# Layer B of a two-layer decoder step: one plain pair of value tiles instead of two, finer steps for the norms ahead of it

## The chip, the core and the metric

One core of a Trainium2 chip runs the whole step in one launch. The metric is the device time of an execution in microseconds. Five engines work from queues of their own: TensorE (PE; its weight loads are PEld), VectorE (DVE), ScalarE (ACT), GpSimd (POOL) and SyncE (SP), which here issues all DMAs. An engine takes its instructions in the order of its queue, and an instruction waits at the head until what it needs is there.

## The reference

Two layers over 1024 prompt tokens and 8 single-token samples, 1032 columns, with a model width of 1024. Layer A is a gated linear recurrence, layer B a gated MLP with spatial mixing. Each layer ends in a per-layer embedding (PLE): a gate from the normed residual times a projection of p.

```python
def chunk_mlp_mixer(h, w_in, ln_g, ln_b, w_sp, b_sp, w_out):
    proj = h @ w_in
    u, v, z = jnp.split(proj, 3, axis=-1)
    u = jax.nn.gelu(u)
    v = layernorm(jax.nn.gelu(v), ln_g, ln_b)
    ...
    y = (u * s * jax.nn.silu(z)) @ w_out
    ...
for i in range(DEPTH):
    hn = rmsnorm(h, norm_mix[i])
    ...
    h = h + y
    gate = jax.nn.sigmoid(rmsnorm(h, norm_ple[i]) @ w_ple_gate[i])
    h = h + gate * (p[i] @ w_ple_proj[i])
```

The change lies where layer A ends and layer B begins: the end of the first gate (i = 0), the second norm of the residual for layer B, the p projection of layer B, and the first tiles of the value branch v.

## The kernel before

**Layout.** Features lie on the partitions, tokens in the free dimension, in three chunks c = 0, 1, 2 of 384, 384 and 264 columns (`OFF`, `W`). A float32 operand is split into a high part in fp32r and a rest (`split`, `split_weights`: the cast is on ACT, the subtraction on DVE or, for every other activation row, on POOL). A product of two such operands is three matmuls (`mm3`: high times high, high times rest, rest times high). A plain output tile of 128 features and one chunk is therefore 8 blocks of depth times 3, or 24 matmuls (`proj`). The split weights of a tile are `whi` and `wlo`, two buffers each, so the cast for the next tile but one waits for the last matmul of the tile that holds the buffer.

**Units.** Most of layer B's input projection runs in units of two output tiles (`unit`): the columns of chunks 0 and 1 and the two halves of the depth make a 2x2 block product, computed by Winograd's scheme in seven products of 12 matmuls instead of eight. Chunk 2 is done plainly (`last`). A unit needs sums of weight blocks (`load_unit`: s1 to s4, four sums on POOL and four more splits `shi`, `slo`), sums of the normed rows (`mix`: the tiles xm, `xmh` and `xml`, three of them, made on DVE from the rows of chunks 0 and 1), and the sum `hr[0][j+4]`, split into the first half of chunk 1's normed tile once its plain readers are done. The first two pairs of value tiles run plainly, because the sums do not exist yet.

**Order.** PE's order is the order in which the code is written. Side work is written as generators, and `tk.tick()` advances all of them by a step; a generator that yields a number sleeps for so many steps. So the number of steps between two pieces decides how many matmuls stand between them in PE's queue. In `proj` there was a step after the fourth of eight blocks, and callers add one at the end of a group: two steps per group of 24. On ACT, DVE, POOL and SP a scheduler sets the order from what the code issues and its priorities.

**The norm between the layers.** When a chunk's last two gate groups are written (`ple`, the pair with m = 6 and 7), `norm_rows` is spawned for that chunk with two numbers from `NDEL[1]`. After the first, `norm_sum` writes small matmuls (`pss`) that sum the squares over the partitions, an addition on DVE (`rms_e`) and a power on POOL (`rsq`). After the second, `norm_bc` writes the matmuls that spread the result over the partitions (`pbc`), and then the eight rows of the chunk are scaled on DVE, cast on ACT (`bh`) and subtracted on DVE and POOL in turns (`bl`). The sum of squares `ssq` of a chunk gets its last addend on DVE (from `sql`, a square on ACT).

**What stands around it on PE.** The last pair of gate tiles; the first half of layer B's p projection (`pple`: 12 products of 6 matmuls, each copied out by ACT as `pple_t` and stored), then the plain value pairs, then the units. The loop around `pple` gave a step for every other product:

```python
for i, _ in enumerate(pple(1, ph, pl, 0, places([(pq, "pple_t", 8)]))):
    if i % 2:
        tk.tick()
```

Behind the first plain pair, a loop ticked until all `norm_rows` were done, and `mix` was spawned there; behind the second, a loop ticked until `mix` was done, and the first unit's weights were loaded.

Of the kernel before, what the change touches and what calls it, by code (L numbers as in the profile page):

```python
# [24 lines left out]
MI = DI // P  # L25
# [11 lines left out]
DL = 4  # L37
KB = 1
SDEL = ((6, 3), (6, 2), (4, 2))
NDEL = (((1, 2), (1, 3), (2, 2)), ((2, 2), (2, 4), (3, 3)))  # L40
OFF = (0, 384, 768)
W = (384, 384, 264)
NT = (3, 3, 2)
CH = (0, 1, 2)
# [36 lines left out]
def trunk_kernel(ctx, tc, xT, st, pT, nrm, wina, lbl, gna, wouta, winb, lng, lnb, lngr, lnbr,  # L81
# [5 lines left out]
    tk = Ticks()  # L87
# [33 lines left out]
    order = [("p", 0, 0)]  # L121
# [7 lines left out]
    order += [("oa", m, f) for m, f in half_order]  # L129
    order += [("g", 0, m) for m in range(KT)]  # L130
    order += [("p", 1, 0)]
    order += [("b", MI + m) for m in range(4)] + [("B", MI + m) for m in range(4, MI, 2)]
    for g in range(8):
        order += [("B", 2 * g), ("B", 2 * MI + 2 * g)]
    order += [("p", 1, 1)]
# [7 lines left out]
    def split_weights(src, width, names, pl):  # L143
        hi = pl.tile([P, width], F32R, name=names[0], **names[2])
        lo = pl.tile([P, width], F32R, name=names[1], **names[2])
        A.copy(hi, src)  # L146
        V.tensor_tensor(lo, src, hi.bitcast(F32), ALU.subtract)  # L147
        return hi, lo
# [6 lines left out]
    def fetch_weights(n):  # L155
        src = wsrc[order[n][0]]
        for i in order[n][1:]:
            src = src[i]
        staged[n] = wp.tile([P, 1024], F32, name="wstg")
        nc.sync.dma_start(staged[n], src)  # L160

    def load(n, wait=False):
        if n >= len(order) or n in loaded or wait and order[n][0] == "B":
            return
        if order[n][0] == "B":
            loaded[n] = load_unit(order[n][1])
            return
        if n not in staged:
            fetch_weights(n)
        stg = staged.pop(n)  # L170
        with tc.high_priority(offset=PRI if order[n][:2] == ("p", 1) or order[n][0] == "b" else 0):
            loaded[n] = split_weights(stg, 1024, PLAIN, wp)
# [27 lines left out]
    taken = [0]  # L200

    def take(*key):
        n = taken[0]
        assert order[n] == key, (order[n], key)
        load(n)
        load(n + 1, key[0] == "b")
        taken[0] += 1
        return loaded[n]


    last, rest = {}, {}

    def split(hi, lo, src, eng=V):
        last["split"] = A.copy(hi, src)  # L214
        last["lo"] = eng.tensor_tensor(lo, src, hi.bitcast(F32), ALU.subtract)  # L215
# [82 lines left out]
    def proj(wt, xh, xl, c):  # L298

        wh, wl = wt  # L300
        ps = pp.tile([P, 512], F32, name="ps_proj", tag="mm", bufs=3)
        for k in range(KT):
            mm3(ps[:, :W[c]], blk(wh, k), blk(wl, k), xh[:, k, :], xl[:, k, :], k == 0, k == KT - 1)
            if k == 3:
                tk.tick()
        return ps

# [9 lines left out]
    def places(stg):  # L317

        n = [0]

        def place(c, mm):
            pl_, tag, bufs = stg[n[0] % len(stg)]
            n[0] += 1
            return pl_.tile([P, 384], F32, name="pple_t", tag=tag, bufs=bufs)[:, :W[c]]
        return place

    def pple(l, ph, pl, half, place):

        wh, wl = take("p", l, half)
        for c in CH:  # L330
            for mm in range(4):
                ps = pp.tile([P, 512], F32, name="ps_pple", tag="mm", bufs=3)
                for k in range(2):
                    b = 2 * mm + k
                    mm3(ps[:, :W[c]], blk(wh, b), blk(wl, b), ph[c][:, k, :], pl[c][:, k, :], k == 0, k == 1)
                t = place(c, mm)
                with tc.high_priority(offset=PRI if l else 0):
                    last["pple"] = A.copy(t, ps[:, :W[c]])  # L338
                nc.sync.dma_start(ppd[l][4 * half + mm][:, OFF[c]:OFF[c] + W[c]], t)
                yield 1  # L340
# [73 lines left out]
    hh, hl = new_act()  # L414
# [11 lines left out]
    ph, pl = [None] * 3, [None] * 3  # L426
# [406 lines left out]
    ph, pl = r["p"]  # L833
# [106 lines left out]
    def ple(l, ep, hh, hl, ssq, done, mid=None):  # L940
        def group(m, c, wg, pj):
            w = W[c]
            pg = proj(wg, hh[c], hl[c], c)
            gt = sp.tile([P, 384], F32, name="tmp", bufs=4)
            with tc.high_priority(offset=PRI if m >= KT - 2 else 0):
                A.activation(gt[:, :w], pg[:, :w], AF.Sigmoid)
                V.tensor_tensor(gt[:, :w], gt[:, :w], pj[:, OFF[c]:OFF[c] + w], ALU.mult)
                V.tensor_tensor(hr[c][m], hr[c][m], gt[:, :w], ALU.add)
            accum_sq(sp, ssq[c], hr[c][m], m == 0, m == KT - 1, w)
            if l == 0:  # L950
                nc.sync.dma_start(hd[m][:, OFF[c]:OFF[c] + w], hr[c][m])
            tk.tick()

        def start(m):
            pj = ep.tile([P, T], F32, name="pj", bufs=2)
            nc.sync.dma_start(pj, ppd[l][m])
            return take("g", l, m), pj

        def pair(m):
            a, b = start(m), start(m + 1)  # L960
            for c in CH:
                group(m, c, *a)
                group(m + 1, c, *b)
                if m == KT - 2:
                    done(c)

        pair(0)
        for m in range(2, KT - 2):
            if m == 3 and mid:
                mid()  # L970
            a = start(m)
            for c in CH:
                group(m, c, *a)
        pair(KT - 2)

    def norm_spawn(c, ssq, gi, act, d):
        tk.spawn(norm_proc(sp, ssq[c], lambda j: hr[c][j], gi, act[0][c], act[1][c], c, d[c]))
# [2 lines left out]
    act = new_act()  # L980
    out_phase("oa", zt, ssq, True, lambda c: norm_spawn(c, ssq, 1, act, NDEL[0]), pre,
              [(c, 8, 8) for c in CH], [(c, 8) for c in CH])
# [21 lines left out]
    def mix():  # L1004


        for j in range(4):
            b11, b12, b21, b22 = hr[0][j], hr[1][j], hr[0][j + 4], hr[1][j + 4]
            with tc.issue_after(last["norm"].ins):
                V.tensor_tensor(b11, b12, b11, ALU.subtract)  # L1010
                V.tensor_tensor(b12, b22, b12, ALU.subtract)
                V.tensor_tensor(b22, b22, b11, ALU.subtract)
                V.tensor_tensor(b21, b21, b22, ALU.subtract)
                for i, t in ((1, b22), (0, b11), (2, b12)):
                    split(xm[i][0][:, j, :], xm[i][1][:, j, :], t)
            yield 1

    with ExitStack() as sG:
        ep = pool(sG, "pj")
        ssq2 = new_ssq()  # L1020
        hn = new_act()
        with ExitStack() as s:
            pq = pool(s, "p1", side="right")
            ph, pl = [None] * 3, [None] * 3

            def mid():
                behind = last["split"]
                for c in CH:
                    load_p(pq, 1, c, ph, pl, behind, [x[:, :2, :W[c]] for x in xm[c]])

            ple(0, ep, act[0], act[1], ssq2, lambda c: tk.spawn(norm_rows(c, ssq2, 2, hn, NDEL[1][c])), mid)
            for i, _ in enumerate(pple(1, ph, pl, 0, places([(pq, "pple_t", 8)]))):
                if i % 2:
                    tk.tick()
    hh, hl = hn

    ws[0] = pool(sB, "wsum")
# [11 lines left out]
    def vgroup(m, c, src, d=2):  # L1049
        w = W[c]  # L1050
        gv = wide()
        A.activation(gv[:, :w], src, AF.Gelu_apprx_tanh)
        if c == 2:
            G.tensor_copy(gvs[:, m, :], gv[:, 256:264])
        tk.spawn(vstore(m, c, gv), d)
# [13 lines left out]
        yield  # L1069


    for q in range(0, 4, 2):
        wv = take("b", MI + q), take("b", MI + q + 1)
        for c in CH:
            for m in range(2):
                ps = proj(wv[m], hh[c], hl[c], c)
                vgroup(q + m, c, ps[:, :W[c]], 4)
                tk.tick()
        if q == 0:
            while any(p[2].__name__ == "norm_rows" for p in tk.procs):  # L1080
                tk.tick()
            tk.spawn(mix(), 1)
    while any(p[2].__name__ == "mix" for p in tk.procs):
        tk.tick()
    for j in range(4):
        split(hh[1][:, j, :], hl[1][:, j, :], hr[0][j + 4])
    load(taken[0])
    sH.close()

    wb2 = pool(sB, "workB2", side="right")  # L1090
# [94 lines left out]
        if not early:  # L1185
            last(1)

    for m in range(4, MI, 2):
        unit(take("B", MI + m), lambda i, c, src: vgroup(m + i, c, src), early=m == 4)

    mv = wb.tile([P, 8, 2], F32, name="mv")
    ss_ = wb2.tile([P, MI, NS], F32, name="ss_")
# [90 lines left out]
    for g in range(8):  # L1283
# [15 lines left out]
        else:  # L1299
# [3 lines left out]
            ph, pl = p_in_act(1, None, False)  # L1303
# [13 lines left out]
            def first():  # L1317
# [8 lines left out]
    act3 = new_act()  # L1326
    out_phase("ob", zt, ssq3, False, lambda c: norm_spawn(c, ssq3, 3, act3, NDEL[0]), {},
              [(1, 12, 4), (2, 0, 8)], [[(2, 0), (2, 8)], [(0, 8), (1, 8), (1, 12)]], pple(1, ph, pl, 1, lambda c, mm: hr[c][4 + mm]))
# [106 lines left out]
```

## Time and profile before

| what | value |
|---|---|
| median of three runs | 1916.89 us |
| the three runs | 1912.62, 1918.22, 1916.89 us |
| the profiled execution's own time | 1914.28 us |
| its span, first to last instruction | 1912.4 us |
| mean granted clock of TensorE | 0.993 |
| DVE, ACT, POOL busy | 60%, 42%, 23% of the span |

A row of the timeline gives the start in us from the span's start, the duration, the engine, the line, the operation, output and inputs, their shapes and how many were merged; in brackets stands the idle time of the engine before it and what ended it. A row of the windows gives for each engine its busy time in that stretch with the number of instructions, then the granted clock and the DMA share. Matmuls are pipelined, so a matmul's duration is longer than the distance to the next one's start; what it costs is that distance.

### The profile page before, as it was taken

How to read it: one execution, taken by the hardware profiler on the slowest of the kernel's cores; microseconds unless marked ns; L12 is line 12 of the kernel's file. 1: busy time of each engine (PE TensorE's matmuls, PEld its weight loads, DVE VectorE, ACT ScalarE, POOL GpSimd, SP SyncE). 2: the span in 40 equal slices, each digit the busy share in tenths (PEclk: the TensorE clock that was granted, in tenths of full speed). 3: DMA queues.
4: the chain of work that ended last, by engine and by line, in shares of the span. 5: the costliest groups of instructions: out<-in, count | busy, mean ns of one | idle time of the engine just before them, and what ended most of it. 6: DMA issues, size and time to landing. Idle time of an engine off the chain costs nothing.

```text
span 1912.4 us, 33713 instructions
## 1 busy us (share of the span) xinstructions
PE 1882.9 (98%) x13250; PEld 1856.2 (97%) x13250; DVE 1156.3 (60%) x2610; ACT 800.1 (42%) x1711; POOL 432.8 (23%) x441
## 2 busy tenths in 40 slices
PE   9999999999999999999999999999999999999997
PEld 8999999999999998999999999999999999999997
DVE  5967676766767677411465755577777776311455
ACT  6463544444454546311244544434434335311342
POOL 4110000000010001011233332345445451011321
PEclk8999999999999999999999999999999999999998
DMA  6231323222231326711243343323333236611123
GB/s 214 76 117 61 118 72 103 78 81 78 92 99 60 111 69 191 251 49 51 76 143 117 109 145 99 90 81 106 124 114 106 97 108 197 222 45 45 67 89 111
DMA packets 124302, 203.76 MB, mean 107 GB/s; under 512 B 11568, under 2 KB 97264, under 8 KB 123120
## 3 DMA queue, kind: packets, MB, share of 16 engines
q1 hardware_dynamic: 124144, 201.61, 32.2%
q8 instruction: 104, 1.70, 0.4%
q14 instruction: 54, 0.44, 0.1%
HBM read 148.75 MB, written 52.82 MB: 105 GB/s over the span
## 4 chain that ended last, share of the span: by engine, by line
PE 90%; DVE 5%; DMA 2%; POOL 1%; ACT 1%; issue 1%; SPq 0%; DVEq 0%; ACTq 0%; POOLq 0%
PE ps_proj L219 18%; PE ps_proj L221 18%; PE ps_proj L220 18%; PE ps_o L219 6%; PE ps_o L220 6%; PE ps_o L221 6%; PE ps_d L221 1%; PE ps_d L219 1%; PE ps_d L220 1%; PE psp L1255 1%; PE pC L672 1%; PE pt_o L718 1%; PE p L638 1%; PE pt_g L1061 1%; PE pss L269 1%
## 5 line engine op out<-in xcount | busy, mean ns | idle before, releaser
L219 PE MATMUL ps_proj<-bh,whi 128*128 128x384 f32 (+1 forms) x2160 | 695.1, 322 | 2.1 <-ACT pple_t L338 1.6
L221 PE MATMUL ps_proj<-bh,wlo 128*128 128x384 f32 (+1 forms) x2160 | 679.9, 315 | 0.5 <-DVE wlo L147 0.5
L220 PE MATMUL ps_proj<-bl,whi 128*128 128x384 f32 (+1 forms) x2160 | 678.8, 314 | 1.4 <-POOL bl L215 1.4
L219 PEld LDWEIGHTS ps_proj<-bh,whi 128*128 128x128 f32 x2160 | 407.4, 189 | 3.6 <-ACT pple_t L338 1.7
L220 PEld LDWEIGHTS ps_proj<-bl,whi 128*128 128x128 f32 x2160 | 407.8, 189 | 2.6 <-POOL bl L215 2.6
L221 PEld LDWEIGHTS ps_proj<-bh,wlo 128*128 128x128 f32 x2160 | 406.5, 188 | 1.7 <-DVE wlo L147 1.7
L147 DVE TENSOR_TENSOR wlo<-wstg,whi 128x1024 fp32r<-128x1024 f32 x148 | 184.8, 1249 | 147.4 <-ACT whi L146 146.2
L146 ACT CAST whi<-wstg 128x1024 fp32r<-128x1024 f32 x148 | 155.0, 1048 | 155.2 <-PE ps_proj L220 104.1
L255 POOL TENSOR_TENSOR ssq<-ssq,tmp 128x384 f32<-128x384 f32 (+1 forms) x72 | 76.3, 1060 | 406.7 <-ACT tmp L254 359.9
L911 DVE TENSOR_TENSOR h<-h,ps_o 128x384 f32<-128x384 f32 (+1 forms) x48 | 24.6, 512 | 192.4 <-PE ps_o L221 190.9
L254 ACT ACTIVATE tmp<-h 128x384 f32<-128x384 f32 (+1 forms) x72 | 35.3, 491 | 219.3 <-DVE h L911 168.9
L219 PE MATMUL ps_o<-bh,whi 128*128 128x384 f32 (+1 forms) x384 | 122.1, 318 | 0.0
L220 PE MATMUL ps_o<-bl,whi 128*128 128x384 f32 (+1 forms) x384 | 121.8, 317 | 0.0
L221 PE MATMUL ps_o<-bh,wlo 128*128 128x384 f32 (+1 forms) x384 | 121.8, 317 | 0.0
L146 ACT CAST shi<-ssum 128x512 fp32r<-128x512 f32 x88 | 54.6, 622 | 110.0 <-PE ps_proj L220 60.2
L219 PE MATMUL ps_o<-zh,whi 128*128 128x384 f32 (+1 forms) x288 | 90.1, 313 | 0.0
L220 PE MATMUL ps_o<-zl,whi 128*128 128x384 f32 (+1 forms) x288 | 89.7, 312 | 0.0
L221 PE MATMUL ps_o<-zh,wlo 128*128 128x384 f32 (+1 forms) x288 | 89.7, 312 | 0.0
L215 POOL TENSOR_TENSOR ql<-q,qh 128x384 fp32r<-128x384 f32 (+1 forms) x24 | 22.4, 931 | 254.5 <-ACT qh L214 254.5
L147 DVE TENSOR_TENSOR slo<-ssum,shi 128x512 fp32r<-128x512 f32 x88 | 68.8, 783 | 12.0 <-ACT shi L146 12.0
L675 DVE TENSOR_TENSOR q<-q,t 128x192 f32<-128x192 f32 (+1 forms) x144 | 47.4, 330 | 44.7 <-PE pC L672 38.3
L219 PEld LDWEIGHTS ps_o<-bh,whi 128*128 128x128 f32 x384 | 72.2, 188 | 0.0
(303 smaller groups left out, 3930.5 us busy)
## 6 DMA issues: line engine op xcount, KB each, us to landing
wstg<-in_wina SPq DMA_DIRECT2D x48, 512.0 KB, 3.7
wstg<-in_winb SPq DMA_DIRECT2D x48, 512.0 KB, 3.7
pj<-ppd SPq DMA_DIRECT2D x16, 516.0 KB, 5.2
S<-in_st SPq DMA_DIRECT2D x16, 512.0 KB, 5.4
vb<-vd SPq DMA_DIRECT2D x16, 512.0 KB, 4.6
out_so_s<-S SPq DMA_DIRECT2D x16, 512.0 KB, 3.4
wstg<-in_wouta SPq DMA_DIRECT2D x16, 512.0 KB, 3.5
wstg<-in_wgate SPq DMA_DIRECT2D x16, 512.0 KB, 3.5
```

Source lines behind the costliest of these rows:

```text
L146: A.copy(hi, src)
L147: V.tensor_tensor(lo, src, hi.bitcast(F32), ALU.subtract)
L215: last["lo"] = eng.tensor_tensor(lo, src, hi.bitcast(F32), ALU.subtract)
L219: PE.matmul(ps, wh, xh, start=first, stop=False, skip_group_check=more)
L220: PE.matmul(ps, wh, xl, start=False, stop=False, skip_group_check=more)
L221: PE.matmul(ps, wl, xh, start=False, stop=last, skip_group_check=more)
L254: A.activation(sq[:, :w], src, AF.Square)
L255: eng.tensor_tensor(ssq, ssq, sq[:, :w], ALU.add)
L269: PE.matmul(pss[:, i:i + 1], t[:, o:o + P], ones[:, 0:1], start=j == 0, stop=j == len(parts) - 1)
L638: PE.matmul(blk(p0, i), blk(Y, i), blk(X, i), start=True, stop=True)
L675: V.tensor_tensor(ql[:, :, 1, :], ql[:, :, 1, :], t2[:, :, 0:1].broadcast_to([P, n, lv]), ALU.mult)
L911: V.tensor_tensor(hr[c][m], hr[c][m], ps[:, :W[c]], ALU.add)
```

## The change

The second plain value pair becomes a unit, so layer B now has one plain pair and seven value units. `mix` is spawned at once, ahead of the only plain pair, and both loops that ticked until work was done are gone. The first unit's weights are loaded after the plain pair's first chunk. In the last pair of the first gate, `proj` gives a step after the second, fourth and sixth block, so that with the caller's step a group of 24 has four; the sleeps of `NDEL[1]` are counted in these. Each p product gives a step.

```diff
-NDEL = (((1, 2), (1, 3), (2, 2)), ((2, 2), (2, 4), (3, 3)))
+NDEL = (((1, 2), (1, 3), (2, 2)), ((3, 2), (5, 3), (3, 3)))
...
-    order += [("b", MI + m) for m in range(4)] + [("B", MI + m) for m in range(4, MI, 2)]
+    order += [("b", MI + m) for m in range(2)] + [("B", MI + m) for m in range(2, MI, 2)]
...
-            if k == 3:
+            if k == 3 or fine[0] and k in (1, 5):
                 tk.tick()
...
+        fine[0] = l == 0
         pair(KT - 2)
+        fine[0] = False
...
-            for i, _ in enumerate(pple(1, ph, pl, 0, places([(pq, "pple_t", 8)]))):
-                if i % 2:
-                    tk.tick()
+            for _ in pple(1, ph, pl, 0, places([(pq, "pple_t", 8)])):
+                tk.tick()
...
-    for q in range(0, 4, 2):
-        wv = take("b", MI + q), take("b", MI + q + 1)
-        for c in CH:
-            for m in range(2):
-                ps = proj(wv[m], hh[c], hl[c], c)
-                vgroup(q + m, c, ps[:, :W[c]], 4)
-                tk.tick()
-        if q == 0:
-            while any(p[2].__name__ == "norm_rows" for p in tk.procs):
-                tk.tick()
-            tk.spawn(mix(), 1)
-    while any(p[2].__name__ == "mix" for p in tk.procs):
-        tk.tick()
+    tk.spawn(mix(), 1)
+    wv = take("b", MI), take("b", MI + 1)
+    for c in CH:
+        for m in range(2):
+            ps = proj(wv[m], hh[c], hl[c], c)
+            vgroup(m, c, ps[:, :W[c]], 4)
+            tk.tick()
+        if c == 0:
+            load(taken[0])
     for j in range(4):
         split(hh[1][:, j, :], hl[1][:, j, :], hr[0][j + 4])
-    load(taken[0])
...
-    for m in range(4, MI, 2):
-        unit(take("B", MI + m), lambda i, c, src: vgroup(m + i, c, src), early=m == 4)
+    for m in range(2, MI, 2):
+        unit(take("B", MI + m), lambda i, c, src: vgroup(m + i, c, src), early=m == 2)
```

**First place: DVE, chunk 1's last addend.** In DVE's queue at the end of the first gate, `ssq_11647` is the sum of squares of chunk 1, `h_7_10170` its last gated row, `h_0_10155` to `h_7_10162` are rows of chunk 0. Before:

```order
L947 TENSOR_TENSOR tmp<-tmp,pj 128x384
L948 TENSOR_TENSOR h_7_10170<-h_7_10170,tmp 128x384
L252 TENSOR_TENSOR ssq_11647<-ssq_11647,sql 128x384
L996 SCALAR_TENSOR_TENSOR h_0_10155<-h_0_10155,g_72,pbc 128x384
L996 SCALAR_TENSOR_TENSOR h_1_10156<-h_1_10156,g_72,pbc 128x384
```

and now:

```order
L949 TENSOR_TENSOR tmp<-tmp,pj 128x384
L1001 SCALAR_TENSOR_TENSOR h_5_10160<-h_5_10160,g_72,pbc 128x384
L950 TENSOR_TENSOR h_7_10170<-h_7_10170,tmp 128x384
L1001 SCALAR_TENSOR_TENSOR h_6_10161<-h_6_10161,g_72,pbc 128x384
L147 TENSOR_TENSOR wlo<-wstg,whi 128x1024
L254 TENSOR_TENSOR ssq_11647<-ssq_11647,sql 128x384
```

Chunk 0's scaled rows have moved ahead of chunk 1's addend, and so has the rest `wlo` of the p weights.

**Second place: DVE, chunk 2's `rms_e`.** Further on in DVE's queue, `h_6_10169` and `h_7_10170` are now rows of chunk 1 being scaled, and `rms_e` is that of chunk 2. Before:

```order
L996 SCALAR_TENSOR_TENSOR h_6_10169<-h_6_10169,g_72,pbc 128x384
L272 TENSOR_SCALAR rms_e<-pss 128x3
L215 TENSOR_TENSOR bl_11653<-h_5_10168,bh_11650 128x384
L996 SCALAR_TENSOR_TENSOR h_7_10170<-h_7_10170,g_72,pbc 128x384
L147 TENSOR_TENSOR wlo<-wstg,whi 128x1024
```

and now:

```order
L1001 SCALAR_TENSOR_TENSOR h_6_10169<-h_6_10169,g_72,pbc 128x384
L1001 SCALAR_TENSOR_TENSOR h_7_10170<-h_7_10170,g_72,pbc 128x384
L217 TENSOR_TENSOR bl_11653<-h_5_10168,bh_11650 128x384
L274 TENSOR_SCALAR rms_e<-pss 128x3
L217 TENSOR_TENSOR bl_11653<-h_7_10170,bh_11650 128x384
```

All eight rows of chunk 1 and three of its four rests now stand ahead of chunk 2's `rms_e`; the `wlo` has moved behind chunk 2's rows.

**Third place: PE, chunk 2's `pbc`.** In PE's queue the matmuls that spread chunk 2's result (`rsq_12769` before, `rsq_12729` now) stood half-way through the first plain group of the value pair (`bh_11649` and `bl_11652` are chunk 0's normed rows). Before:

```order
L219 MATMUL ps_proj<-bh_11649,whi 128x384
L220 MATMUL ps_proj<-bl_11652,whi 128x384
L221 MATMUL ps_proj<-bh_11649,wlo 128x384
L280 MATMUL pbc<-ident,rsq_12769 128x128 x2
L280 MATMUL pbc<-ident,rsq_12769 128x8
```

and now (`xmh_11639` and `xml_11640` hold chunk 1 of p here):

```order
L221 MATMUL ps_pple<-xmh_11639,whi 128x384
L222 MATMUL ps_pple<-xml_11640,whi 128x384
L223 MATMUL ps_pple<-xmh_11639,wlo 128x384
L282 MATMUL pbc<-ident,rsq_12729 128x128 x2
L282 MATMUL pbc<-ident,rsq_12729 128x8
```

They have moved ahead of the last five of the twelve p products. In all PE has 12 matmuls of 384 columns fewer.

More of the change, by code (lines that the diff above doesn't have):

```diff
@@ L211, in trunk_kernel @@
     last, rest = {}, {}
+    fine = [False]
     def split(hi, lo, src, eng=V):
@@ L973, in ple @@
                 group(m, c, *a)
+        fine[0] = l == 0
         pair(KT - 2)
+        fine[0] = False
     def norm_spawn(c, ssq, gi, act, d):
@@ L1069, in vstore @@
         yield
-    for q in range(0, 4, 2):
-        wv = take("b", MI + q), take("b", MI + q + 1)
-        for c in CH:
-            for m in range(2):
-                ps = proj(wv[m], hh[c], hl[c], c)
-                vgroup(q + m, c, ps[:, :W[c]], 4)
-                tk.tick()
-        if q == 0:
-            while any(p[2].__name__ == "norm_rows" for p in tk.procs):
-                tk.tick()
-            tk.spawn(mix(), 1)
-    while any(p[2].__name__ == "mix" for p in tk.procs):
-        tk.tick()
+    tk.spawn(mix(), 1)
[7 more added lines that the diff above has]
+            load(taken[0])
+    assert not any(p[2].__name__ in ("norm_rows", "mix") for p in tk.procs)
     for j in range(4):
         split(hh[1][:, j, :], hl[1][:, j, :], hr[0][j + 4])
-    load(taken[0])
     sH.close()
```

## The prediction

> **What bounds the kernel now.** I read the page first, then the chain of work that ended last, then the windows and PE's timeline from the first gate to the first unit, and last the rows of DVE, ACT and POOL there.
>
> ```profile
> span 1912.4 us, 33713 instructions
> PE 1882.9 (98%) x13250; PEld 1856.2 (97%) x13250; DVE 1156.3 (60%) x2610; ACT 800.1 (42%) x1711; POOL 432.8 (23%) x441
> PE 90%; DVE 5%; DMA 2%; POOL 1%; ACT 1%; issue 1%; SPq 0%; DVEq 0%; ACTq 0%; POOLq 0%
> ...
> 1044.00:1060.00 16.00, 14.77 (x97) 13.81 (x96) 13.67 (x25) 11.18 (x26) 9.09 (x9) 1.00 0.59 198
> 1060.00:1070.00 10.00, 10.00 (x62) 10.00 (x61) 9.60 (x18) 6.97 (x15) 5.32 (x6) 1.00 0.46 135
> ...
> 1090.00:1100.00 10.00, 10.00 (x60) 9.68 (x60) 3.32 (x6) 3.60 (x8) 5.51 (x4) 1.00 0.12 36
> ...
> 1140.00:1150.00 10.00, 10.00 (x65) 9.97 (x65) 5.68 (x12) 5.01 (x9) 2.24 (x2) 1.00 0.28 86
> ```
>
> PE is busy for 98% of the span and is 90% of the chain, so a matmul less is time less, as long as PE finds its operands. The windows show where it does not: between 1044 and 1060 us, the p products with the norms, PE stands for 1.23 us and DVE is busy for 13.67 of 16. In the plain pairs (1090 to 1100) and the units (1140 to 1150) PE is full and DVE has room. So the change takes work from a full stage and presses norm work into the one stage where DVE is nearly full.
>
> **What it removes.** A plain pair has 144 matmuls, a unit 84 of 384 columns and 48 of 264: 12 of 384 columns fewer. Their price is the distance of starts, from the first and the last of 41 neighbours:
>
> ```profile
> 1009.77 0.33 PE L220 MATMUL ps_proj<-bl,whi 128*128 128x384 f32 x1
> ...
> 1016.70 0.33 PE L221 MATMUL ps_proj<-bh,wlo 128*128 128x384 f32 x1
> ```
>
> 6.93 us over 40 distances is 0.173 us, and 12 of them are **2.08 us less**. What the unit adds on the other engines (four POOL sums, four more splits) lies beside PE, as the unit window shows; without that cover its DVE and POOL time, some 6 us, would be the price.
>
> **What the norm stage costs.** PE's places and waits before:
>
> ```profile
> 1042.12 0.72 PE L269 MATMUL pss<-ones,ssq 128*128 128x1 f32 x6
> ...
> 1047.20 0.34 PE L221 MATMUL ps_pple<-xmh,wlo 128*128 128x384 f32 x1
> 1047.72 0.45 PE L219 MATMUL ps_pple<-xmh,whi 128*128 128x384 f32 x1 [0.18 <-ACT pple_t L338]
> ...
> 1048.70 0.34 PE L221 MATMUL ps_pple<-xmh,wlo 128*128 128x384 f32 x1
> 1049.22 0.44 PE L219 MATMUL ps_pple<-xmh,whi 128*128 128x384 f32 x1 [0.18 <-ACT tmp L946]
> ...
> 1051.25 0.34 PE L221 MATMUL ps_pple<-xmh,wlo 128*128 128x384 f32 x1
> 1052.45 0.93 PE L280 MATMUL pbc<-ident,rsq 128*128 128x128 f32 x6 [0.87 <-POOL rsq L228]
> ...
> 1118.26 0.42 PE L219 MATMUL ps_proj<-xmh,shi 128*128 128x384 f32 x1
> ```
>
> Three distances are longer than 0.17 us: by 0.35, 0.35 and 1.03, together **1.73 us of old waits**. I let them all go, since the order around them is new, and price the new ones.
>
> ```profile
> 1039.74 0.56 DVE L252 TENSOR_TENSOR ssq<-ssq,sql 128x384 f32<-128x384 f32 x1 [0.72 <-ACT sql L248]
> ...
> 1042.37 1.23 DVE L147 TENSOR_TENSOR wlo<-wstg,whi 128x1024 fp32r<-128x1024 f32 x1
> ...
> 1049.66 2.03 DVE L147 TENSOR_TENSOR wlo<-wstg,whi 128x1024 fp32r<-128x1024 f32 x1
> ...
> 1053.43 2.19 DVE L996 SCALAR_TENSOR_TENSOR h<-h,g,pbc 128x384 f32<-128x384 f32 x4 [0.93 <-PE pbc L280]
> 1055.53 0.57 DVE L215 TENSOR_TENSOR bl<-h,bh 128x384 fp32r<-128x384 f32 x1
> ...
> 1063.33 1.68 DVE L996 SCALAR_TENSOR_TENSOR h<-h,g,pbc 128x264 f32<-128x264 f32 x4
> ...
> 1069.42 1.01 DVE L1010 TENSOR_TENSOR h<-h,h 128x384 f32<-128x384 f32 x2
> ...
> 1085.55 0.53 DVE L215 TENSOR_TENSOR xml<-h,xmh 128x384 fp32r<-128x384 f32 x1
> ...
> 1099.48 0.69 DVE L147 TENSOR_TENSOR slo<-ssum,shi 128x512 fp32r<-128x512 f32 x1 [1.84 <-ACT shi L146]
> ```
>
> ```profile
> 1041.28 1.05 ACT L146 CAST whi<-wstg 128x1024 fp32r<-128x1024 f32 x1
> ```
>
> ```profile
> 1035.86 0.85 POOL L228 TENSOR_TENSOR rsq<-rms_e,mhalf 128x3 f32<-128x3 f32 x1
> ...
> 1050.57 1.83 POOL L228 TENSOR_TENSOR rsq<-rms_e,mhalf 128x3 f32<-128x3 f32 x1
> ...
> 1058.52 1.02 POOL L215 TENSOR_TENSOR bl<-h,bh 128x384 fp32r<-128x384 f32 x1 [1.55 <-ACT bh L214]
> ...
> 1091.20 1.29 POOL L188 TENSOR_TENSOR ssum<-wstg 128x512 f32<-128x512 f32 x1 [3.93 <-DMA vraw<-u]
> ```
>
> *First wait, chunk 1's `pss`.* The same matmuls stand ahead of it as before, so PE reaches it at 1042.1. Its addend was on DVE at 1039.74; now it is behind the p weights' `wlo`, and that behind the cast `whi`, which needs the buffer of gate tile 6, freed by PE 12 matmuls of 264 columns (1.45 us, by columns from 0.173) earlier, at about 1040.7. The row has the cast at 1041.28 with casts of rows ahead of it; now it may begin 0.4 earlier. Cast 1.05, rest 1.23 and addend 0.56 end between 1043.4 and 1044.1; I take 1043.75, a **wait of 1.65 us**. Queued behind the addend are chunk 0's last two rows, and behind the waiting `pss` all of PE. The bounds are 1.3, and 2.8 where the rest costs the 2.03 of the later row.
>
> *Chunk 1's `pbc`* comes one p product later (0.6 + 1.45 + 1.0 us after the `pss`, at 1046.8). Three DVE rows stand ahead of `rms_e` (1.4 us), and `rsq` takes 0.85, so it is ready at about 1046.1: nothing. With 1.83 for `rsq` it costs 0.2.
>
> *Second wait, chunk 2's `pbc`.* PE reaches it after the `pss` (0.6), 12 matmuls of 264 columns (1.45), 42 of p products (7.3), a `pbc` (0.7) and a `pss` of twelve (1.2): 1043.75 + 11.25 = 1055.0. DVE arrives later. The first value tile's `whi` needs gate tile 7's buffer, free at 1045.8; cast and rest end at 1048.1, a gate product (0.4) later chunk 1's rows begin at 1048.5. Ahead of `rms_e` stand eight of them (0.525 each from the row of four, 4.2), three rests (1.5), a gate row (0.4), and I allow 0.8 for a late cast, since ACT also copies the products: 1055.4. POOL's `bl` of row 6 (1.02) goes first, then `rsq` (0.85): 1057.3, a **wait of 2.3 us**. Bounds: 0, if ACT's casts never hold DVE and `bl` is early, and 3.3 with the slow `rsq`.
>
> Sum: -2.08 - 1.73 + 1.65 + 2.3 = **+0.1 us**.
>
> The slow `rsq` of 1050.57 begins inside the `wlo` of 1049.66, which ends at 1051.69, and 0.85 after that is 1052.5, where it ends. [...]
>
> **What is hidden.** `mix` begins when chunk 2's rows are done: 1057.3 + 1.0 for `pbc`, 3.4 for eight rows, 1.7 for rests, 1.2 for a `wlo`, so 1064.6. Before it took from 1069.42 to 1086.1, 16.7 us; now it would end at 1081.3. The weight sums took 9.0 us from the first POOL sum (1091.20) to the end of the last rest (1100.17); placed wholly behind `mix`, they end at 1090.3. PE's first product with xm stood at 1118.26. A pair less (96 x 0.173 + 48 x 0.12 + an estimated 1.4 for 16 transposes and their breaks, 23.8 us) and 2.2 us later in the norm stage make it 1096.7. So there are 6 us of cover; if they go, PE waits one for one.
>
> At the end of layer B the staging tiles change parity: the buffer `wstg3` now holds the last unit's first tile, and two loads of z slices wait for POOL's last use of it.
>
> ```profile
> 1572.77 1.30 POOL L195 TENSOR_TENSOR ssum<-wstg,ssum 128x512 f32<-128x512 f32 x1
> ```
>
> ```profile
> 1589.60 0.51 ACT L363 CAST xmh<-wstg 128x384 fp32r<-128x384 f32 x1
> ```
>
> From 1574.1 to 1589.60 there are 15 us for a load, so I cost it at nothing. SP stands at that load meanwhile; behind it in its queue stand p's second half and the first output weights, both used after 1589.
>
> **The rivals.** *The norms cost nothing new* (22%): ACT's casts run ahead, and `rsq` of chunk 2 is ready. For it speaks that 0.8 of DVE's 6.9 us ahead of `rms_e` are only my allowance and `bl` may end early; against it, that the addend stands behind `wlo` in any case. -2.08, and at most -3.8 with all waits gone.
>
> *The norms cost more* (11%): slow `wlo` and both slow `rsq` add 0.8 + 2.0, and a wait long enough slows the clock, as this stretch later in the trace shows:
>
> ```profile
> PE ps_pple L219 <- ACT h L338: 3.8, 1, 3.8
> ...
> 1612.00:1615.00 3.00, 3.00 (x12) 3.00 (x11) 0.60 (x1) 0.91 (x2) 0.00 (x0) 0.52 0.81 202
> ```
>
> After a wait of 3.8 us the granted clock was 0.52 for 3 us, a loss of 1.4 us; after the 0.87 at 1052 it stayed at 1.00. That makes +0.1 + 2.8 + 1.4 = +4.3 us. [...]
>
> *The unit comes too early* (8%, slower than before): `mix` and the weight sums are late for the product at 1096.7, one mechanism at one place, PE's first `ps_proj<-xmh,shi`. For it speaks that the whole second pair, 24 us, was its cover, and that POOL's second sum waits for a rest on DVE behind `mix`; against it the 6 us and the DVE idle at 1090 to 1100. It makes the kernel slower from 6 us of delay on, and by more than 0.3% from 11.6 on, about +6 us.
>
> *The steps do not move what bounds* (part of the forecast): the norms get earlier places on PE, but DVE's work is the same, so PE waits at them instead.
>
> **How the numbers follow.** The forecast, from -1.5 to +2, has 53%; the rivals 22%, 11% and 8%; 6% I leave for a gain above 0.3%, for which I know no cause. 0.3% is 5.7 us, about what a measurement of this kernel can tell from no change; the first three cases lie within it. So faster 0.06, same 0.86, slower 0.08. The sum against the profiled execution is 1914.28 + 0.1 = 1914.4; the median of the three runs is 2.6 us higher, and the middle of the four about 1915.6, from which I predict **1915.7**. The range goes from 1914.28 - 3.8 = 1910.5 to 1916.89 + 4.3 = 1921.
>
> **What would show it.** Right: `pss` of chunk 1 with an idle of 1 to 2 us put down to DVE's `ssq`, `pbc` of chunk 2 with 1 to 3 us put down to `rsq`, 12 fewer matmuls, the first xm product near 1096.7 without a wait. Wrong: a wait there put down to `xml`, `slo` or `shi`; a clock below 1.00 between 1040 and 1100; or a new wait after 1570.

## The result and the profile after

| | before | after |
|---|---|---|
| median (22 runs each) | 1914.55 us | 1920.30 us |
| lowest to highest | 1912.02 to 1918.22 us | 1915.75 to 1925.30 us |
| profiled execution, its span | 1914.28, 1912.4 us | 1917.01, 1915.3 us |

The ratio is 1.0031, interval 1.0023 to 1.0038: the changed kernel is **5.75 us slower**, where the prediction had +0.1. The profiled execution is one of the faster ones of the changed kernel; the last section shows what goes with the scatter. Medians are those of all runs; `e8_last_late` and `e11_other_bank` below have one slow run each (2232.85 and 3741.14 us), which their ratios leave out and without which their medians are 1914.39 and 1908.71.

The head of the page:

```profile
span 1915.3 us, 33724 instructions
...
PE 1878.6 (98%) x13238; PEld 1852.5 (97%) x13238; DVE 1162.4 (61%) x2619; ACT 801.9 (42%) x1716; POOL 437.4 (23%) x445
```

PE has the 12 matmuls less, and is 98% busy as before; such a share doesn't show a loss of 0.3%. The waits do. TensorE's between 1015 and 1120 us in the changed kernel (line, what it waited for, us in total, times, longest):

```profile
PE pss L271 <- DVE ssq L254: 2.9, 1, 2.9
PE pt_g L1065 <- ACT u L1067: 2.7, 2, 2.2
PE pbc L282 <- POOL rsq L230: 2.5, 1, 2.5
```

Before, the same stretch had 1.8 us, the two lines here and two waits of `ps_pple` of 0.2; now it has 8.1.

```profile
PE pbc L280 <- POOL rsq L228: 0.9, 1, 0.9
PE pt_g L1061 <- ACT u L1063: 0.5, 1, 0.5
```

The first and the third of the new waits were forecast, the second was not. PE's timeline at the three places:

```profile
1043.59 0.80 PE L271 MATMUL pss<-ones,ssq 128*128 128x1 f32 x6 [2.91 <-DVE ssq L254]
1044.25 0.38 PE L221 MATMUL ps_proj<-bh,whi 128*128 128x264 f32 x1
...
1046.63 0.42 PE L223 MATMUL ps_proj<-bh,wlo 128*128 128x264 f32 x1
1046.85 0.52 PE L221 MATMUL ps_pple<-xmh,whi 128*128 128x384 f32 x1
...
1059.34 0.83 PE L282 MATMUL pbc<-ident,rsq 128*128 128x128 f32 x6 [2.54 <-POOL rsq L230]
...
1088.78 0.44 PE L1065 MATMUL pt_g<-ident,u 128*128 128x128 f32 x1 [2.20 <-ACT u L1067]
```

Behind the first wait the twelve matmuls of 264 columns take 2.60 us (1044.25 to 1046.85); in the kernel before they took 1.54 (1042.71 to 1044.25). The windows say why; the column behind the five engines' busy times is the granted clock. Each row is 3.41 us long: the one with a wait, then the next.

```profile
1041.09:1044.50 3.41, 0.91 (x8) 0.94 (x9) 3.41 (x5) 1.18 (x5) 1.00 (x1) 1.00 0.50 172
1044.50:1047.91 3.41, 3.41 (x16) 3.41 (x16) 1.22 (x4) 1.53 (x3) 1.03 (x1) 0.50 0.21 79
1054.74:1058.15 3.41, 2.06 (x12) 1.73 (x11) 1.97 (x6) 2.98 (x7) 2.00 (x3) 1.00 0.34 124
1058.15:1061.56 3.41, 2.22 (x16) 2.22 (x17) 1.77 (x5) 0.83 (x3) 1.47 (x3) 1.00 0.16 58
1085.45:1088.87 3.42, 1.22 (x11) 1.01 (x10) 3.15 (x5) 1.85 (x5) 1.64 (x1) 1.00 0.00 0
1088.87:1092.28 3.41, 3.41 (x16) 3.41 (x17) 3.41 (x9) 1.64 (x4) 2.22 (x1) 0.50 0.71 204
```

The waits of 2.9 and 2.2 us are each followed by 3.4 us at a clock of 0.50; the one of 2.5 us is not. At 0.50 the matmuls of 264 columns start 0.22 us apart instead of 0.12, so a row at half clock and full of work costs an estimated 1.5 to 1.7 us of its 3.41.

**Where the time is, end to end.** The same three matmuls in both traces: the last of layer A's output, the first product with xm, the first product of layer B's second p half.

```profile
947.96 0.28 PE L221 MATMUL ps_o<-zh,wlo 128*128 128x264 f32 x1
...
1118.26 0.42 PE L219 MATMUL ps_proj<-xmh,shi 128*128 128x384 f32 x1
...
1604.01 0.33 PE L219 MATMUL ps_pple<-bh,whi 128*128 128x384 f32 x1
```

```profile
946.44 0.28 PE L223 MATMUL ps_o<-zh,wlo 128*128 128x264 f32 x1
...
1101.56 0.42 PE L221 MATMUL ps_proj<-xmh,shi 128*128 128x384 f32 x1
...
1609.59 0.33 PE L221 MATMUL ps_pple<-bh,whi 128*128 128x384 f32 x1
```

From the first to the second: 170.3 us before, 155.1 now. A pair less should have taken 23.8 off (the prediction's figure, of which 1.4 for the transposes is an estimate that no row shows; the second pair's 144 matmuls and its transposes took 24.8 in the trace of before, 1084.12 to 1108.88), so by that figure this stage lost 8.6. From the second to the third: 485.75 before, 508.03 with one unit more, so a unit is 22.3 us and gains 1.5 on the pair's 23.8 (forecast 2.08). Together **+7.1 us** up to the second p half. Behind it the profiled execution is 2.7 us shorter (1915.3 - 1609.59 against 1912.4 - 1604.01), because the wait on ACT's `h` there is 2.8 us instead of 3.8 and no half clock followed it this time. The shorter wait is not chance: it is 3.8 and 3.7 us in the two kernels profiled with two plain pairs, and 2.0 to 2.8 in all eleven profiles with one. Ahead of 946 the execution is 1.5 shorter, in code that the change leaves alone. That makes the 2.9 of the two spans.

### The profile page after: what moved, and what is told of

Same layout as the page of the kernel before. It is cut to its first block, busy times and chain, and to the rows that moved or that the text cites. A ratio compares the mean times of both kernels' runs of the same rounds, so it can differ in the third digit from the quotient of the medians.

```text
span 1915.3 us, 33724 instructions
## 1 busy us (share of the span) xinstructions
PE 1878.6 (98%) x13238; PEld 1852.5 (97%) x13238; DVE 1162.4 (61%) x2619; ACT 801.9 (42%) x1716; POOL 437.4 (23%) x445
## 5 line engine op out<-in xcount | busy, mean ns | idle before, releaser
L221 PE MATMUL ps_proj<-bh,whi 128*128 128x384 f32 (+1 forms) x2136 | 687.2, 322 | 2.5 <-ACT pple_t L340 1.6
L223 PE MATMUL ps_proj<-bh,wlo 128*128 128x384 f32 (+1 forms) x2136 | 672.2, 315 | 1.2 <-DVE wlo L147 1.0
L222 PE MATMUL ps_proj<-bl,whi 128*128 128x384 f32 (+1 forms) x2136 | 671.2, 314 | 1.1 <-POOL bl L217 0.6
L146 ACT CAST whi<-wstg 128x1024 fp32r<-128x1024 f32 x148 | 155.1, 1048 | 160.6 <-PE ps_proj L222 108.4
L217 POOL TENSOR_TENSOR ql<-q,qh 128x384 fp32r<-128x384 f32 (+1 forms) x24 | 22.3, 928 | 254.4 <-ACT qh L216 254.4
```

The lines of the kernel that those rows point to most:

```text
L221: PE.matmul(ps, wh, xh, start=first, stop=False, skip_group_check=more)
L222: PE.matmul(ps, wh, xl, start=False, stop=False, skip_group_check=more)
L223: PE.matmul(ps, wl, xh, start=False, stop=last, skip_group_check=more)
```

## The experiments

Three batches, each beside the kernel before on the same chip (medians 1914.34, 1914.44 and 1914.53 us).

### Which half of the change costs: the steps or the second pair

The change has two halves, the unit in place of a pair and the new steps of the norms. Two runs do one half each. `e1_old_steps` has one plain pair with the steps, sleeps and places of before, and `mix` begins when all `norm_rows` are done:

```diff
-NDEL = (((1, 2), (1, 3), (2, 2)), ((3, 2), (5, 3), (3, 3)))
+NDEL = (((1, 2), (1, 3), (2, 2)), ((2, 2), (2, 4), (3, 3)))
...
-        fine[0] = l == 0
+        fine[0] = False
...
-            for _ in pple(1, ph, pl, 0, places([(pq, "pple_t", 8)])):
-                tk.tick()
+            for i, _ in enumerate(pple(1, ph, pl, 0, places([(pq, "pple_t", 8)]))):
+                if i % 2:
+                    tk.tick()
...
+        yield lambda: not any(p[2].__name__ == "norm_rows" for p in tk.procs)
         for j in range(4):
```

> The changed kernel with the old steps: no finer steps in the last gate pair, the old numbers for the norms, a step for every other p product; mix starts once the norms are written. Theory A (the norms' new places make PE wait, and the waits bring half clock): the waits at chunk 1's pss (2.9 us) and chunk 2's pbc (2.5) go, the time falls to 0 to 2 us above the kernel before. Theory B (one plain pair is too little cover for mix and the weight sums): the waits go too, but mix starts later, so the wait at the transposes of the plain pair stays or grows and the time stays 4 to 7 us above before.

`e2_two_pairs` has both plain pairs of before and the new `NDEL[1]`, the finer steps and the step for each p product.

> The kernel before with the finer steps, the new numbers for the norms and a step for each p product, and two plain pairs kept. Theory A: 4 to 7 us slower than before, with both norm waits of the changed kernel. Theory B: within 2 us of before.

| median us (ratio to before, interval) | old steps | new steps |
|---|---|---|
| two plain pairs | 1914.34 | 1921.29 (1.0025, 1.0013 to 1.0037) |
| one plain pair | 1912.97 (0.9989, 0.9978 to 1.0000) | 1920.30 (1.0031, 1.0023 to 1.0038) |

By the medians the steps add 7.0 to 7.3 us with either number of pairs, and the intervals of the two columns lie apart. So the steps of the norms are the whole loss. The unit takes 1.0 to 1.4 us off by the medians, but within each column the intervals overlap or touch, so its gain is not shown. Between 1015 and 1120 us `e2_two_pairs` has the same two waits and no other, and half clock behind both (3.4 us from 1046.6, 6.8 us from 1060.3):

```profile
PE pss L271 <- DVE ssq L254: 2.9, 1, 2.9
PE pbc L282 <- POOL rsq L230: 2.5, 1, 2.5
```

### Is it the unit's cover, or where the norms stand

`e3_load_late` moves `load(taken[0])` behind the plain pair, so that the weight sums stand behind it. `e4_norms_late` leaves that alone and gives chunk 1's `pss` and chunk 2's `pbc` later places:

```diff
-NDEL = (((1, 2), (1, 3), (2, 2)), ((3, 2), (5, 3), (3, 3)))
+NDEL = (((1, 2), (1, 3), (2, 2)), ((3, 2), (9, 3), (3, 9)))
```

> The changed kernel with the first unit's weights loaded behind the plain pair, as before, so that ACT's casts of the weight sums stand behind the pair's copies of transposes. Theory A: the two norm waits stay, 0 to 2 us less than the changed kernel. Theory B: the wait of 2.2 us at the transposes and the half clock behind it go, 3 to 4 us less than the changed kernel.

> The changed kernel with other numbers for the norms only: chunk 1 (9, 3) instead of (5, 3), chunk 2 (3, 9) instead of (3, 3), so that chunk 1's pss stands behind the second p product and chunk 2's pbc half-way through the first plain group, where it was before. Theory A: both waits and the half clock behind them go, 4 to 7 us less than the changed kernel, at or below before. Theory B: 0 to 2 us less.

`e3_load_late`: 1920.54 us, ratio 1.0027 (1.0016 to 1.0038). The `pt_g` wait fell from 2.7 to 0.5, and waits on `whi` (2.0) and `wlo` (1.3) came in its place: no gain, where theory B had 3 to 4 us. `e4_norms_late`: 1915.50, ratio 1.0007 (0.9995 to 1.0019), most of the loss gone with the late places, as theory A had it.

### Which of the norms' places

> The changed kernel with chunk 0's norm put back to its old places on TensorE (pss 12 matmuls later, pbc 24 later); chunk 1's and chunk 2's norms stay at the new, earlier places, and everything else is the changed kernel. In VectorE's queue chunk 1's last addend to ssq then stands ahead of chunk 0's scaled rows and of the rest wlo again. Theory C (the largest single loss is chunk 1's pss, which waits 2.9 us because chunk 0's earlier norm pushed its addend back, and which brings 1.7 us of half clock behind it): no wait of pss on ssq above 1 us, no half clock at 1044 to 1048, the wait of chunk 2's pbc on rsq still above 1.5 us; about 1920.3 - 4.6 = 1915.7 us. Rival D (the loss is chunk 2's pbc with the half clock behind it): pbc waits 2.5 us or more and the time stays at 1918 to 1920. Rival E (VectorE is simply full in this stage, so a wait that goes comes back at the next place): the waits of this stage sum up to 6 us or more as in the changed kernel, 1919 to 1921.

> The changed kernel with chunk 2's pbc alone put back to its old place, half-way through the first plain value group (30 matmuls later). Theory C: pss of chunk 1 still waits 2.9 us with half clock behind it; the pbc of chunk 2 waits under 0.5 us; the time falls by that wait and what half clock comes behind it, 2 to 3 us, to about 1918. Rival D: the time falls by 4 us or more, to 1916 or less, though pss still waits. Rival E: another wait of 2 us or more appears behind it (pt_g, whi, or the first group's bl), 1919 to 1921.

```diff
-NDEL = (((1, 2), (1, 3), (2, 2)), ((3, 2), (5, 3), (3, 3)))
+NDEL = (((1, 2), (1, 3), (2, 2)), ((5, 4), (5, 3), (3, 3)))
```

is `e7_first_late`, and in `e8_last_late` the last group reads `((3, 2), (5, 3), (3, 9))`.

`e7_first_late` took 1926.36 us, ratio 1.0061 (1.0049 to 1.0074): **theory C fell**. The `pss` wait went, as it said, and something worse came. PE, DVE and POOL in that run:

```profile
1049.31 1.65 PE L282 MATMUL pbc<-ident,rsq 128*128 128x128 f32 x6 [6.95 <-POOL rsq L230]
```

```profile
1046.12 0.15 DVE L274 TENSOR_SCALAR rms_e<-pss 128x3 f32<-128x3 f32 x1
...
1046.53 2.01 DVE L147 TENSOR_TENSOR wlo<-wstg,whi 128x1024 fp32r<-128x1024 f32 x1
```

```profile
1047.43 1.83 POOL L230 TENSOR_TENSOR rsq<-rms_e,mhalf 128x3 f32<-128x3 f32 x1
```

Chunk 0's rows now come later on DVE, so chunk 1's `rms_e` stands behind them until 1046.12. Then its `rsq` is the slow one (1.83 beside a `wlo` of 2.01), and chunk 1's `pbc`, left at its early place, waits 6.95 us. Chunk 2's still waits 3.18. DVE's work between the norms is the limit; a place on PE earlier than DVE can serve it is a wait, whichever chunk has it. That is rival E in its mechanism, for the waits of chunks 0 and 1; its 1919 to 1921 us was 5 us too low.

`e8_last_late` took 1914.58 us, ratio 1.0001 (0.9991 to 1.0011): **the move of chunk 2's `pbc` alone takes 5.7 us off**, as rival D had it. Yet the wait of `pss` is the same, with its half clock:

```profile
PE pss L271 <- DVE ssq L254: 2.9, 1, 2.9
PE ps_proj L223 <- DVE wlo L147: 1.6, 1, 1.6
PE pt_g L1065 <- ACT u L1067: 0.5, 1, 0.5
```

```profile
1058.82 1.17 POOL L230 TENSOR_TENSOR rsq<-rms_e,mhalf 128x3 f32<-128x3 f32 x1
```

```profile
1063.31 0.73 PE L282 MATMUL pbc<-ident,rsq 128*128 128x128 f32 x6
```

`rsq` is ready at 1059.99, and PE comes to it at 1063.31. PE's 30 matmuls ahead of `pbc` run while DVE and POOL work, instead of behind them. The order on ACT moves a little with this edit: the copies of `pt_g` stand better to the casts `shi`, and the wait there falls to 0.5. So the 5.7 hold that wait too (2.2 us), beside the 2.5 of `pbc` and the half clock at 1088.9, less the wait on `wlo` that came (1.6). Against `e1_old_steps`, which has the unit and neither norm wait, it is 1.6 us more by the medians, which these runs can't tell apart.

### Is the half clock caused by the wait

`e9_filled` writes 18 small matmuls into an unused part of the `pss` tile while PE waits for chunk 1's addend. The other engines' order is that of the changed kernel but for a swap of neighbours on DVE (chunk 1's `rms_e` comes two places later), ACT and POOL.

```diff
+        if c == 1 and last.pop("fillq", 0):
+            for i in range(18):
+                PE.matmul(pss[:, 256:384], ones[:, 0:1].broadcast_to([P, P]), ident, start=True, stop=True)
         for i in range(cols):
```

> The changed kernel with 18 additional small matmuls (128x128, written into an unused part of the pss tile and overwritten by nothing that is read) ahead of chunk 1's pss, to keep TensorE busy while it waits for ssq; the order on the other engines is unchanged. It leaves no part of the result out. Theory F (the half clock at 1044.5 is caused by TensorE standing idle for 2.9 us): the wait shrinks to under 0.8 us, the pss starts at the same time as before, 1043.6, the 12 matmuls of 264 columns behind it take 1.45 us instead of 2.60 and the records show no half clock from 1044 to 1048; about 1.7 us less, 1918.6 us. Rival G (the clock follows from something else than this gap, or such small matmuls do not count as work): the half clock at 1044 to 1048 stays, 1920.3 us.

The two windows at the same place:

```profile
1040.60:1044.01 3.41, 3.41 (x33) 3.41 (x32) 3.41 (x5) 1.17 (x5) 1.01 (x1) 1.00 0.48 167
1044.01:1047.42 3.41, 3.41 (x29) 3.41 (x27) 1.34 (x5) 2.08 (x4) 1.56 (x2) 1.00 0.22 84
```

PE is full in the first, and the clock in the second is 1.00. Without the filler an estimated 2.5 us of the first would have been idle (from 1040.60 to the end of `ssq`, 1042.93 in this run, and the 0.15 to the `pss`), so the place of the windows isn't what differs. The twelve matmuls of 264 columns behind it take 1.54 us instead of 2.60. So theory F holds on the cause: with PE filled in place of the gap, the clock was 1.00 instead of 0.50. The time, 1919.38 us (ratio 1.0027, 1.0016 to 1.0038), is 0.9 below the changed kernel, not 1.7, and within what these runs can't tell apart: the filler took 4.0 us for a wait of 2.9 and put `pss` 1.0 us later, reckoned from the last matmul of layer A's output (946.44 and 945.83 us): 97.2 us behind it in the changed kernel, 98.2 here.

### Is the pt_g wait a loss of its own

`e12_after_bank` is the changed kernel with the second tile's `pt_g` in another PSUM buffer (`tag="po" if m == 1 else "pt"`), and nothing moves on any engine.

> The changed kernel with the same other buffer for every second pt_g of the plain pair and nothing else; the order on all engines is that of the changed kernel. Theory H: the pt_g waits of 2.7 us go, with them the half clock behind the one of 2.2 us where it came, 1920.3 - 2.2 - 1.0 = about 1917 us. Rival I: the wait moves to another operand of the plain pair, 1919 to 1920 us. The waits of pss (2.9 us) and pbc (2.5 us) stay in either case.

1921.46 us, ratio 1.0038 (1.0026 to 1.0050): no gain. The `pt_g` waits are gone, and in the same stretch stand

```profile
PE pss L271 <- DVE ssq L254: 2.9, 1, 2.9
PE pbc L282 <- POOL rsq L230: 2.5, 1, 2.5
PE ps_proj L223 <- DVE wlo L147: 2.0, 1, 2.0
PE ps_proj L221 <- ACT whi L146: 1.5, 1, 1.5
```

The wait has moved to `wlo` and `whi`, as rival I said (its 1919 to 1920 us was 1.5 us too low). As `e3_load_late` and this run read, the whole plain pair of the changed kernel runs ahead of what DVE, ACT and POOL have done; which operand is missing first is secondary.

### A version that beats both

`e10_both_kept` is `e1_old_steps` with the unit's weights loaded behind chunk 1 of the plain pair (`if c == 1:`), and `e11_other_bank` adds the other buffer for `pt_g`.

> One plain pair, the norms at the places and steps of the kernel before (as in the run that kept the old steps), and the first unit's weights loaded behind chunk 1 of the plain pair instead of chunk 0, so that ScalarE's copies of the transposed values stand ahead of the casts shi. If the pt_g wait of 1.9 us (and the half clock behind it at 1087) is what this stage still loses: pt_g waits under 0.7 us, no half clock there, first product with xm without a wait; 1912.97 - 1.2 - 1.7 = about 1910 to 1911 us. Rival: the sums come later and the first shi product waits instead by 2 us or more; 1913 to 1915 us.

> The fastest version so far (one plain pair, old places of the norms, the unit's weights loaded behind chunk 1), with the transposes pt_g of the second tile of each plain pair in the PSUM buffer that pss used, so that two pt_g no longer share one buffer; the order on all engines is the same. Theory H (the pt_g wait of 1.7 us there is a loss of its own): it falls under 0.3 us, no other wait grows, 1912.28 - 1.5 = about 1910.8 us. Rival I (TensorE runs into the next late thing instead, a ps_proj buffer or whi, behind the same casts on ScalarE): the wait moves, 1912 to 1913 us.

`e10_both_kept`: 1912.28 us, ratio 0.9986 (0.9977 to 0.9995); `pt_g` still waited 1.7 us, so the later load did not do what was expected of it, and from `e1_old_steps` (0.9989) the runs can't tell it. `e11_other_bank`: **1909.08 us, ratio 0.9975 (0.9965 to 0.9984)**, 5.5 us faster than before and 11 faster than the changed kernel. Its longer waits in the stretch:

```profile
PE ps_proj L223 <- DVE wlo L147: 1.7, 1, 1.7
PE pbc L282 <- POOL rsq L230: 0.9, 1, 0.9
```

By the medians the other buffer gained 3.2 us here and nothing in `e12_after_bank`. That this gain comes from the edit is not shown. `e10_both_kept` ran in another batch, on another chip, and the two intervals overlap. In the profiles the stage of the edit takes the same time; here are the last matmul of layer A's output and the first product with xm, in `e10_both_kept` and in `e11_other_bank`:

```profile
952.91 0.28 PE L223 MATMUL ps_o<-zh,wlo 128*128 128x264 f32 x1
...
1101.59 0.42 PE L221 MATMUL ps_proj<-xmh,shi 128*128 128x384 f32 x1
```

```profile
945.22 0.28 PE L223 MATMUL ps_o<-zh,wlo 128*128 128x264 f32 x1
...
1093.86 0.42 PE L221 MATMUL ps_proj<-xmh,shi 128*128 128x384 f32 x1
```

That is 148.68 and 148.64 us. The `pt_g` waits are gone, but behind the wait on `wlo` the second profile has 3.4 us at half clock (from 1084.35) that the first has not. The 7.7 us by which it is ahead lie before layer A's last output, in code that both share. That `e11_other_bank` is faster than the kernel before is clear of the noise; which part of it the buffer gave stays open.

### The changed kernel once more

> The changed kernel once more, for a second profile of it. Theory J (the clock is judged in fixed windows of 3.41 us: where TensorE stands for 1.9 us or more within one of them, the next one runs at half clock; all windows of the ten profiles so far with 2.0 us or more of idle were followed by half clock, and of 33 with 1.0 to 1.8 us only two): the waits are the same (2.9, 2.5, 2.2 us), but since the windows fall elsewhere in this execution, half clock may now miss one of the waits that had it and hit chunk 2's pbc, and in each case the rule holds. Rival K (the length of a wait alone decides): half clock behind the same two waits as in the first profile, pss and pt_g, and again none behind pbc.

1918.60 us. The waits were the same to the tenth. Half clock came again behind `pss` (1046.1) and behind `pt_g` (1090.5), and not behind `pbc`, whose wait fell once more into two windows. So this run holds for J and for K alike; what speaks against K is `e3_load_late`, in which the same wait of 2.5 us ahead of `pbc` lies in one window:

```profile
1058.31:1061.73 3.42, 1.14 (x7) 0.81 (x5) 1.40 (x4) 2.10 (x5) 2.93 (x3) 1.00 0.46 173
1061.73:1065.14 3.41, 3.15 (x12) 3.15 (x13) 1.66 (x5) 0.81 (x2) 0.85 (x2) 0.50 0.00 0
```

Here PE stood for 2.3 us within the window, and the next one is at 0.50. In the changed kernel the wait was split, 1.35 and 1.19 us, and both following windows stayed at 1.00. K falls. `e3_load_late` is one of the ten profiles from which J was formed; in the three taken after that (`e11_other_bank`, `e12_after_bank`, `e13_same_again`) all nine windows with 1.9 us or more of idle had half clock behind them, as J said.

## Why the prediction was wrong

**Right.** Both new waits came where they were put and on what they were put down to: `pbc` of chunk 2 with 2.5 us on `rsq` (forecast 2.3), `pss` of chunk 1 on `ssq`. That the second has its forecast size is partly luck: PE came to it at 1056.80 and `rsq` ended at 1059.28, 3.3 and 3.5 us later behind layer A's last output than forecast, so both ends were late together. The unit gains about 1.5 of the 2.08 us in the profile, with the estimate in the 23.8, and the old waits went. The end of layer B cost nothing; its wait on `h` even became 1 us shorter. The first product with xm had no wait of its own. Luck again is that the forecast time of 1915.7 us misses 1920.30 by only 4.6: its base, from four runs, was 1.0 above the median of the 22.

**The step that failed first** is that the sum prices no half clock behind the two new waits of 1.65 and 2.3 us. The prediction's two rows, a wait of 3.8 us with half clock behind it and one of 0.87 without, leave all between them open; that waits of this size are too short for it was not shown. In the profile waits of 2.9 and 2.2 us brought about 1.6 us each. Behind the first: 1.06 on twelve matmuls of 264 columns and 0.5 on the first matmuls of the p products. This is the missing term, about +3.2, and `e9_filled` shows its cause (clock 1.00 once PE was filled). The forecast's own sign for being wrong, "a clock below 1.00 between 1040 and 1100", is what came.

The profile of before already had half clock behind less idle than 3.8 us. At the windows' edges (last section) the wait ahead of the row at 1612 falls into 1.42 us (1605.32 to 1608.73, a clock of 1.00 behind it) and 2.42 us (1608.73 to 1612.14, 0.50 behind it), so no window was without work. And at 750 us, in layer A, a wait of 2.35 us has half clock behind it:

```profile
751.74 0.49 PE L718 MATMUL pt_o<-ident,on 128*128 128x128 f32 x2 [2.35 <-DVE ss_e L712]
```

```profile
751.98:755.39 3.41, 3.41 (x14) 3.31 (x13) 3.07 (x8) 2.99 (x9) 0.39 (x1) 0.50 0.89 239
```

**The first wait was mis-sized**, 2.9 for 1.65, above even its bound of 2.8. PE came to `pss` when it should have (at 1040.68, 94.2 us behind layer A's last output, as before), and the cast `whi` began as early as forecast (1039.15, that is 92.7 behind it); the addend was late:

```profile
1038.16 1.36 DVE L949 TENSOR_TENSOR tmp<-tmp,pj 128x384 f32<-128x384 f32 x1
...
1040.97 1.21 DVE L147 TENSOR_TENSOR wlo<-wstg,whi 128x1024 fp32r<-128x1024 f32 x1
1042.10 1.34 DVE L254 TENSOR_TENSOR ssq<-ssq,sql 128x384 f32<-128x384 f32 x1
```

```profile
1038.09 1.02 POOL L217 TENSOR_TENSOR bl<-h,bh 128x384 fp32r<-128x384 f32 x1 [0.27 <-ACT bh L216]
...
1042.03 1.00 POOL L217 TENSOR_TENSOR bl<-h,bh 128x384 fp32r<-128x384 f32 x1 [2.92 <-ACT bh L216]
```

The two DVE rows that cost 0.56 each in the trace of before took 1.36 and 1.34. Each began 0.07 us behind the start of a `bl` on POOL and ended 0.41 us after that `bl`; why, no run shows. Beyond the 0.56 the two took 1.6 us, more than the 1.25 that was missing; with the prediction's own lower bound of 1.3 it makes the 2.9. The prediction weighed such slow rows for `rsq` and `wlo` alone (1.83 for 0.85, 2.03 for 1.23), where it should have gone over every DVE row beside a POOL row.

**"So there are 6 us of cover" overlooked ACT.** It was reckoned up to the first product with xm, and that held. But ACT's queue serves the plain pair too:

```profile
1084.62 1.14 ACT L146 CAST shi<-ssum 128x512 fp32r<-128x512 f32 x2 [1.14 <-POOL ssum L190]
...
1087.73 0.62 ACT L146 CAST shi<-ssum 128x512 fp32r<-128x512 f32 x1 [1.57 <-POOL ssum L195]
1088.25 0.47 ACT L1067 COPY u<-pt_g 128x384 f32<-128x384 f32 x1
```

The cast `shi` stood waiting for POOL's sum, and behind it the copy that frees `pt_g`: 2.2 of the 2.7 us on PE. `e3_load_late` and `e12_after_bank` show that this term is not free-standing. Taken away, it came back as waits on `whi` and `wlo`.

**The sum as measured**, in the profiled execution and up to the second p half: unit -1.5, old waits -1.73 and -0.5 (`pt_g`), new ones 2.9 + 2.5 + 2.7, half clock 3.2 gives +7.6 against the +7.1 of the three matmuls. The rest of 0.5 us isn't assigned. The medians lie 3.0 us further apart than the two profiled executions (5.75 against 2.73), and the last section shows that the changed kernel's slower runs have the lower mean clock.

**Which of the rivals.** "The norms cost more" named the mechanism, half clock behind a longer wait, and gave it 11% and +4.3; the price came out at +5.75. Its other conditions did not come: the `wlo` ahead of the addend took 1.21 us, and the two `rsq` 1.03 and 1.16. Two `rsq` of 1.83, 0.98 us more each, would also be the +2 at the top of the forecast's range, and the traces show one at most where POOL was followed: chunks 1 and 2 had 1.83 and 0.85 before, 1.83 and 1.17 in `e7_first_late`. The forecast also took 0.3% for about the least that can be told from no change; with 22 runs of each kernel the interval is 0.08% to either side. What all the sums missed is that the terms are not independent. Within one trace they add up, but an edit that takes one away does not take its size off: the waits of one stage stand for the same lateness of DVE. `e8_last_late` kept the `pss` wait and took as long as the kernel before, `e7_first_late` took it away and lost 6 more. The question was not how long each norm waits, but how many matmuls PE still has ahead of chunk 2's `pbc`, the last of the stage that DVE fills.

## What to carry to other kernels

Where a second engine is nearly full in a stage, count PE's work ahead of the last result it must deliver there, and place that use late; earlier places give PE nothing to do and put it to waiting. Here a wait of 2.2 us on PE cost nearly twice its length, with a clock of 0.50 behind it, and one of 2.5 us, split into 1.35 and 1.19 us by a window's edge, did not. To learn whether a wait is a loss of its own, take it away without moving anything else (another buffer, as here): if it comes back under another name, the stage is limited elsewhere. Where the time falls, compare the same two matmuls on both sides of the edit in both traces, before the gain is put down to it.

## What the runs showed of the hardware

**The stretches at half clock began at multiples of 3.4133 us from one another, and one followed every such length that had 1.9 us or more of idle.** In each of the 13 profiles the multiples hold to within 0.01 us over the whole execution: in the changed kernel at 750.9, 1044.5 and 1088.9, 86 and 13 such lengths apart, in the kernel before at 752.0 and 1612.1, 252 apart. Dividing each profile into windows of this length and adding up the time without a matmul in each (windows that begin between 35 and 1895 us, full clock in the window itself) gives:

| idle in a window | windows | next one at half clock |
|---|---|---|
| below 1.2 us | 6978 | 4, all 39 to 45 us from the start |
| 1.2 to 1.8 us | 25 | 4 |
| 1.8 to 1.9 us | 4 | 1 |
| 1.9 to 2.0 us | 7 | 7 |
| 2.0 us and more | 24 | 24 |

The ends of matmuls are modelled in a profile, so the bounds between the rows are not sharp. By the table half clock goes with the idle in one window, and the length of a wait alone does not tell it: the wait of 2.5 us ahead of chunk 2's `pbc` had it in two of the six profiles that show this wait (`e2_two_pairs` and `e3_load_late`; not in the changed kernel, `e9_filled`, `e12_after_bank` and `e13_same_again`). The place of the windows differs between executions: of the changed kernel's two profiles one has a window from 1044.5 us, the other from 1046.1.

That fits the scatter of the changed kernel's times, from 1915.75 to 1925.30 us. One window at 0.50 takes 3.41 x 0.5 / 1917 = 0.0009 off the mean clock of an execution. Of the 22 runs the ten with a mean clock of 0.991 to 0.994 took 1915.75 to 1919.68 us, the twelve with 0.987 to 0.990 took 1920.14 to 1925.30. Which waits the windows hit in the runs without a profile is not on record.
